# Moving the transposes of the merged branch sum behind the next twelve products in a two-layer mixer kernel

## Chip, cores and metric

The program runs on one core of one Trainium2 chip. The metric is the device time of one execution in microseconds (us); lower is better. TensorE (PE) does the matrix products and the transposes, VectorE (DVE) and ScalarE (ACT) the elementwise work, SyncE (SP) issues the loads of weights.

## What is computed

Two blocks follow one another, each with two layers, on 256 tokens of width 1024. Only the end of each layer of the second block matters here:

```python
merged = None
for n, yb in enumerate((y_hg, y_cf, y_sc, y_at, y_mem)):
    term = jax.nn.sigmoid(h @ w_gate[l, n]) * (yb @ w_branch[l, n])
    merged = term if merged is None else merged + term
x = x + rmsnorm(merged @ w_out[l], norm_post[l])
```

So five gated branches are summed into `merged` (256 x 1024), and the sum is multiplied by a 1024 x 1024 matrix.

## The kernel before, in words

Every large product is done in three passes on split operands: a value is cut into a high part (`wh`, `hh`, `yh`, `mh`) and a low part (`wl`, `hl`, `yl`, `ml`), and `mm3` adds high x high, high x low and low x high in PSUM (lines L527 to L529). The split of a tile is an ACT copy (high part) and a DVE subtraction (low part): L313 and L314 for weights, L533 and L534 (`split`) for activations. Weights arrive as 1 MB tiles `raw` from SP (L292), with three tiles in flight, and three pairs `wh`/`wl` in use. `ws.pace()` issues two half tiles of splitting after each step.

A branch is four steps of `chunk5` for the columns 0 to 511 (i = 0) and four for 512 to 1023 (i = 1). A step `part(q, t)` is twelve products, 4 slices of the contraction by 3 passes, each 128 x 512: q says which half of the contraction (one weight tile each), t which 128 of the 256 tokens. In the order of the branches the steps are (q, t) = (0,0), (0,1), (1,0), (1,1). A step with q = 1 finishes a gate and calls its `evac`, here `after(i)`: ACT takes tanh of the gate (`th`, L1725), PE multiplies the branch by its 1024-wide matrix (`br`, six products), DVE forms the term (L1736) and adds it to `m` (L1737), the token-major sum.

In the last branch (`pos == 4`) the sum is complete after each such call. It has to be transposed, since the product with `w_out` contracts over its columns: PE transposes 4 squares of 128 x 128 into one PSUM bank `tr` (L1742), and `split` makes `mh` and `ml` of them. I call these four groups of four transposes the turns: the first turn is (t, i) = (0, 0), the second (1, 0), the third (0, 1), the fourth (1, 1). Each layer has four, so the kernel has eight. Behind the fourth come the steps of the product with `w_out`, from `mh` and `ml`, in the order (0,0), (1,0), (0,1), (1,1) for the first 512 columns (`t_first=True`).

A scheduler places the instructions; on each engine they then run in the order that it has written.

Of the kernel before, what the change touches and what calls it, by code (L numbers as in the profile page):

```python
# [18 lines left out]
P = 128  # L19
# [327 lines left out]
def build(tc, a, out, dbg=None, stop=None):  # L347
# [11 lines left out]
    act, dve, pe = nc.scalar, nc.vector, nc.tensor  # L359

    def bank(name="ps"):
        return pp.tile([P, 512], F32, name=name, tag="ps")
# [5 lines left out]
    def row_bcast(ap, n):  # L368
        return bass.AP(tensor=ap.tensor, offset=ap.offset, ap=[[0, P], [1, n]])
# [17 lines left out]
    ident = cstt[:, 0:128]  # L387
# [3 lines left out]
    def pc(name, j=0, n=1):  # L391
        return pcol[:, PO[name] + j:PO[name] + j + n]
# [133 lines left out]
    def mm3(o, ah, al, bh, bl, start, stop):  # L526
        pe.matmul(o, ah, bh, start=start, stop=False, skip_group_check=True)  # L527
        pe.matmul(o, ah, bl, start=False, stop=False, skip_group_check=True)  # L528
        pe.matmul(o, al, bh, start=False, stop=stop, skip_group_check=True)  # L529

    def split(h, lo, src):

        act.activation(h, src, AF.Copy)  # L533
        dve.tensor_tensor(lo, src, h.bitcast(F32), op=OP.subtract)  # L534
# [91 lines left out]
    def views(key, nk=KD):  # L626
        wh, wl = ws.get(S[key])
        return (wh.rearrange("p (k c) -> p k c", k=nk), wl.rearrange("p (k c) -> p k c", k=nk))
# [16 lines left out]
    def chunk_steps(key, form, xs, evac):  # L645
# [3 lines left out]
        def half(i):  # L649
            def f():  # L650
                if i == 0:
                    box["ps"] = bank("mm").rearrange("p (i c) -> p i c", i=2)
                    box["w"] = views(key)
                for k in range(KD):
                    grp_k(box["ps"][:, i, :], form, box["w"], xs, i, k, KD, i == 0 and k == 0)
                if i == 1:
                    ws.done(S[key])
                    evac(box["ps"])
                ws.pace()
            return f  # L660
        return [half(0), half(1)]

    def chunk5(keys, xs, evac, t_first=False):


        box = {}

        def part(q, t):
            def f():
                if q == 0:  # L670
                    box[t] = bank("mm")
                wh, wl = views(keys[q], 4)
                ts = slice(t * P, (t + 1) * P)
                for k in range(4):
                    j = 4 * q + k
                    mm3(box[t], xs[0][:, j, ts], xs[1][:, j, ts], wh[:, k, :], wl[:, k, :], j == 0, j == 7)
                if t == 1:
                    ws.done(S[keys[q]])
                if q == 1:
                    evac(t, box[t])  # L680
                ws.pace()
            return f
        return [part(q, t) for t in range(2) for q in range(2)] if t_first else [
            part(q, t) for q in range(2) for t in range(2)]
# [262 lines left out]
    def mixer(l):  # L947
# [180 lines left out]
        steps = []  # L1128
        steps += chunk_steps(("w1", l, 6), "A", H, ev_misc)
        steps += chunk5([("w1", l, 2), ("w1", l, 3)], H, ev_q("a"))  # L1130
        steps += chunk5([("w1", l, 4), ("w1", l, 5)], H, ev_vf)
        for c in range(2):
            steps += chunk_steps(("w1", l, 7 + c), "B", H, ev_to(qf[:, 2 * c:2 * c + 2, :], 0.125))
# [217 lines left out]
    def layer2(l, st):  # L1351
# [312 lines left out]
        kmajor5([keys["hf_f"], keys["hf_b"]], H2, ev_f)  # L1664
        steps = []
        steps += chunk5([keys["hi"], keys["akv"]], H2, ev_hi)
        steps += chunk_steps(keys["hq"], "B", H2, evs["hq"][1])
        steps.append(lambda: active.append(hgrn()))
# [9 lines left out]
        m = ap_.tile([P, 2, 1024], F32, name="m")  # L1678
        ap3 = tc.tile_pool(name="at3", bufs=1)
        ap3_ = ap3.__enter__()  # L1680
        mm_box = []
# [4 lines left out]
        def finish(g):  # L1686
            if g in active:
                for _ in g:
                    pass
                active.remove(g)  # L1690

        def branch_steps(pos, n):
            box = {}

            def begin():
                if n in (3, 4):
                    finish(gens["at"])
                if n == 1:
                    finish(gens["cf"])
                if pos == 4:  # L1700
                    ap3.__exit__(None, None, None)
                    mp = tc.tile_pool(name="mh2", bufs=1)
                    mp_ = mp.__enter__()
                    mm_box.extend([mp, mp_.tile([P, KD, T], F32R, name="mh"), mp_.tile([P, KD, T], F32R, name="ml")])
                    gb = mp_.tile([P, 1024], F32, name="gb")
                    nc.scalar.dma_start(gb, row_bcast(a["npost"][l:l + 1], 1024))
                    xt = x_tok
                    if l == 0:
                        xt = mp_.tile([P, 2, 1024], F32, name="xt")
                        for t in range(2):  # L1710
                            for q in range(2):
                                b = bank("tr")
                                for j in range(4):
                                    pe.transpose(b[:, j * P:(j + 1) * P], x[:, 4 * q + j, t * P:(t + 1) * P], ident)
                                act.activation(xt[:, t, q * 512:(q + 1) * 512], b, AF.Copy)
                    mm_box.extend([xt, gb])
                yh = ap_.tile([P, 2, T], F32R, name="yh", bufs=1)
                yl = ap_.tile([P, 2, T], F32R, name="yl", bufs=1)
                split(yh, yl, sz[YN[n]])
                box["y"] = (yh, yl)  # L1720

            def after(i):
                def f(t, ps):
                    th = ap_.tile([P, 512], F32, name="th", bufs=2)
                    act.activation(th, ps, AF.Tanh, scale=0.5)  # L1725
                    b = bank("br")
                    wh, wl = views(("wbr", l, n), 2)
                    yh, yl = box["y"]
                    ts, s = slice(t * P, (t + 1) * P), slice(i * 512, (i + 1) * 512)
                    for k in range(2):  # L1730
                        mm3(b, yh[:, k, ts], yl[:, k, ts], wh[:, k, s], wl[:, k, s], k == 0, k == 1)
                    mm = m[:, t, s]
                    if pos == 0:
                        dve.scalar_tensor_tensor(mm, th, 1.0, b, op0=OP.add, op1=OP.mult)
                    else:
                        dve.scalar_tensor_tensor(th, th, 1.0, b, op0=OP.add, op1=OP.mult)  # L1736
                        dve.tensor_tensor(mm, mm, th, op=OP.add)  # L1737
                    if pos == 4:
                        mh, ml = mm_box[1:3]
                        b = bank("tr").rearrange("p (k c) -> p k c", k=4)  # L1740
                        for k in range(4):
                            pe.transpose(b[:, k, :], m[:, t, i * 512 + k * P:i * 512 + (k + 1) * P], ident)  # L1742
                        split(mh[:, 4 * i:4 * i + 4, ts], ml[:, 4 * i:4 * i + 4, ts], b)
                    if i == 1 and t == 1:
                        ws.done(S["wbr", l, n])
                return f
            out_ = []
            for i in range(2):
                cs = chunk5([("wgate", l, n, 2 * i), ("wgate", l, n, 2 * i + 1)], H2, after(i))
                if i == 0:  # L1750
                    first = cs[0]

                    def f0(first=first):
                        begin()
                        first()
                    cs[0] = f0
                out_ += cs
            return out_
# [8 lines left out]
        mp, mh, ml, xt, gb = mm_box  # L1767
# [33 lines left out]
        if l == 0:  # L1801

            mem_kv(1)
            with tc.high_priority(HP):
# [4 lines left out]
                for k in range(KD):  # L1809
                    g, b = pc("npre1", k), bs[k // 2][:, k % 2, :]  # L1810
# [31 lines left out]
```

## Time and profile before

| | |
|---|---|
| median of 3 runs | 1530.48 us (1529.31 to 1531.53) |
| the profiled execution | 1530.64 us, of which its span is 1528.7 us |
| PE busy, weight loads busy | 1457.7 us (95%), 1301.0 us (85%) |
| DVE, ACT busy | 1123.4 us (73%), 783.9 us (51%) |
| TensorE clock granted, mean over the span | 0.983 of full speed |

The span is the time from the first to the last instruction of the profiled execution. A busy share is an average over stages; which engine sets the end is read from the waits and from the chain of work that ended last.

### The profile page before, as it was taken

The numbers are of one execution on the slowest core, as the hardware profiler recorded it, in microseconds if no ns is written. First come the engines' busy times: TensorE is split into PE (matmuls) and PEld (weight loads), VectorE is DVE, ScalarE is ACT, GpSimd is POOL, SyncE is SP. The second block draws the span as 40 slices with busy tenths as digits, with TensorE's granted clock in tenths as the row PEclk, the third lists the DMA queues.
The fourth block names the chain that finished last, engine by engine and source line by source line (L and its number), as shares of the span: only waits on it lengthen the run. The fifth ranks groups of instructions, "written<-read, shape, count | busy, mean of one in ns | idle before, by whom it ended". The sixth has DMA issues, their size and how long they took to land.

```text
span 1528.7 us, 24737 instructions
## 1 busy us (share of the span) xinstructions
PE 1457.7 (95%) x10036; PEld 1301.0 (85%) x10036; DVE 1123.4 (73%) x1983; ACT 783.9 (51%) x1310; POOL 18.0 (1%) x21
## 2 busy tenths in 40 slices
PE   3999998999989999999999999999998999999997
PEld 1688797999978887989999999987886898977875
DVE  7887565798977876778866777976665759976654
ACT  2655543655655555465555564346454754455442
POOL 0000000000000000000000000000000000000000
PEclk9999999999999999999999999999999999999999
DMA  9567534678744665557655352254553542435541
GB/s 366 204 237 268 193 138 143 248 267 297 263 165 138 248 221 193 193 195 270 228 191 194 138 193 101 95 191 139 182 217 116 215 160 89 159 117 181 190 165 55
DMA packets 42451, 289.21 MB, mean 189 GB/s; under 512 B 4993, under 2 KB 6145, under 8 KB 8034
## 3 DMA queue, kind: packets, MB, share of 16 engines
q1 hardware_dynamic: 39456, 281.77, 51.4%
q10 hardware_dynamic: 2882, 5.88, 1.1%
q8 instruction: 78, 1.28, 0.3%
q14 instruction: 35, 0.29, 0.1%
HBM read 285.53 MB, written 2.10 MB: 188 GB/s over the span
## 4 chain that ended last, share of the span: by engine, by line
PE 80%; DVE 6%; DMA 2%; ACT 2%; issue 1%; POOL 1%; DVEq 0%; POOLq 0%; ACTq 0%; SPq 0%
PE mm L528 20%; PE mm L527 19%; PE mm L529 19%; PE acc L528 2%; PE acc L529 2%; PE acc L527 2%; DVE wl L314 1%; PE br L529 1%; PE br L527 1%; PE br L528 1%; DVE cc L1626 1%; PE S L1477 1%; PE tr L781 1%; ACT wh L313 1%; PE ex L1498 1%
## 5 line engine op out<-in xcount | busy, mean ns | idle before, releaser
L314 DVE TENSOR_TENSOR wl<-raw,wh 128x1024 fp32r<-128x1024 f32 x428 | 515.3, 1219 | 183.4 <-ACT wh L313 180.8
L313 ACT ACTIVATE wh<-raw 128x1024 fp32r<-128x1024 f32 x428 | 440.2, 1054 | 345.8 <-PE mm L528 212.7
L528 PE MATMUL mm<-hl,wh 128*128 128x256 f32 x1568 | 451.2, 288 | 0.0
L527 PE MATMUL mm<-hh,wh 128*128 128x256 f32 x1568 | 448.1, 286 | 2.3 <-ACT wh L313 2.3
L529 PE MATMUL mm<-hh,wl 128*128 128x256 f32 x1568 | 448.0, 286 | 2.2 <-DVE wl L314 2.2
L528 PEld LDWEIGHTS mm<-hl,wh 128*128 128x128 f32 x1568 | 302.3, 193 | 8.2 <-issue 7.1
L527 PEld LDWEIGHTS mm<-hh,wh 128*128 128x128 f32 x1568 | 302.3, 193 | 6.2 <-ACT wh L313 2.5
L529 PEld LDWEIGHTS mm<-hh,wl 128*128 128x128 f32 x1568 | 302.1, 193 | 3.7 <-DVE wl L314 3.0
L528 PE MATMUL mm<-wl,hh 128*128 128x512 f32 (+1 forms) x496 | 194.9, 393 | 0.0
L527 PE MATMUL mm<-wh,hh 128*128 128x512 f32 (+1 forms) x496 | 192.9, 389 | 1.1 <-ACT hh L598 1.1
L529 PE MATMUL mm<-wh,hl 128*128 128x512 f32 (+1 forms) x496 | 192.0, 388 | 1.6 <-DVE hl L534 1.6
L528 PEld LDWEIGHTS mm<-wl,hh 128*128 128x128 f32 x496 | 94.3, 190 | 23.3 <-issue 4.5
L527 PEld LDWEIGHTS mm<-wh,hh 128*128 128x128 f32 x496 | 94.5, 191 | 21.1 <-ACT hh L598 1.4
L529 PEld LDWEIGHTS mm<-wh,hl 128*128 128x128 f32 x496 | 94.4, 190 | 19.6 <-DVE hl L534 1.8
L418 DVE SCALAR_TENSOR_TENSOR raw<-raw,cbp 128x1024 f32<-128x1024 f32 x80 | 96.1, 1218 | 9.5 <-DMA raw<-in_modw 9.3
L528 PE MATMUL acc<-zl,wh 128*128 128x256 f32 x352 | 98.3, 280 | 0.6 <-DVE zl L534 0.6
L529 PE MATMUL acc<-zh,wl 128*128 128x256 f32 x352 | 98.5, 280 | 0.0
L527 PE MATMUL acc<-zh,wh 128*128 128x256 f32 x352 | 98.4, 281 | 0.0
L528 PEld LDWEIGHTS acc<-zl,wh 128*128 128x128 f32 x352 | 66.3, 188 | 1.0 <-DVE zl L534 1.0
L527 PEld LDWEIGHTS acc<-zh,wh 128*128 128x128 f32 x352 | 66.0, 188 | 0.2
L529 PEld LDWEIGHTS acc<-zh,wl 128*128 128x128 f32 x352 | 66.1, 188 | 0.0
L752 ACT ACTIVATE p<-lg,nm 128x256 f32<-128x256 f32 (+1 forms) x80 | 33.5, 430 | 46.3 <-DVE nm L749 46.3
(409 smaller groups left out, 2073.1 us busy)
## 6 DMA issues: line engine op xcount, KB each, us to landing
raw<-in_w SPq DMA_DIRECT2D x70, 1024.0 KB, 4.9
raw<-in_wup SPq DMA_DIRECT2D x44, 1024.0 KB, 4.9
raw<-in_modw SPq DMA_DIRECT2D x40, 1024.0 KB, 5.0
raw<-in_wgate SPq DMA_DIRECT2D x40, 1024.0 KB, 4.8
raw<-in_wdn SPq DMA_DIRECT2D x22, 1024.0 KB, 4.8
raw<-in_wo SPq DMA_DIRECT2D x16, 1024.0 KB, 4.8
raw<-in_wbr SPq DMA_DIRECT2D x10, 1024.0 KB, 4.8
gst<-in_modw SPq DMA_DIRECT2D x8, 1024.0 KB, 12.7
```

Of the source, the lines that this page charges most:

```text
L313: nc.scalar.activation(h[:, s], r[:, s], AF.Copy)
L314: nc.vector.tensor_tensor(lo[:, s], r[:, s], h[:, s].bitcast(F32), op=OP.subtract)
L418: dve.scalar_tensor_tensor(v, v, 1.0, cb_box[0], op0=OP.mult, op1=OP.mult, accum_out=col)
L527: pe.matmul(o, ah, bh, start=start, stop=False, skip_group_check=True)
L528: pe.matmul(o, ah, bl, start=False, stop=False, skip_group_check=True)
L529: pe.matmul(o, al, bh, start=False, stop=stop, skip_group_check=True)
L752: act.activation(p4[:, h, 0:nk], src[:, i, 0:nk], AF.Exp, bias=nm[:, h:h + 1], accum_out=su[:, h:h + 1])
L781: pe.transpose(b[:, h, :], p4[:, h, kt * P:(kt + 1) * P], ident)
L1477: pe.matmul(b[par][:, 2 * s + ft, :], kt[r, ft, s * P:(s + 1) * P], qt[r, ft, t * P:(t + 1) * P], start=True, stop=True, skip_group_check= ...
L1498: pe.matmul(o, g[:, d, t, ft * P:(ft + 1) * P], cols[0], start=(t == 0 and n == 0), stop=(n == 1), skip_group_check=True)
L1626: dve.scalar_tensor_tensor(c[:, ft, :], u[:, ft, k:k + T], w, c[:, ft, :], op0=OP.mult, op1=OP.add)
```

## The change

The transposes of a turn and the split of what they give become a function `turn`, put on a list `late` and called by the next step of `chunk5`, after its twelve products and ahead of its `evac`. The first and the third turn were scheduled into the middle of the following step's products before; now they stand behind all twelve. The second turn stood directly behind the six `br` products that complete its sum; now the first step (0,0) of the columns 512 to 1023 stands between. The fourth turn goes behind the first step of the product with `w_out`, which needs only tokens 0 to 127 and columns 0 to 511, that is the first turn's result. No operation is added or taken away.

```diff
+    late = []
+
     def chunk5(keys, xs, evac, t_first=False):
...
                 if t == 1:
                     ws.done(S[keys[q]])
+                while late:
+                    late.pop(0)()
                 if q == 1:
                     evac(t, box[t])
                 ws.pace()
...
                     if pos == 4:
-                        mh, ml = mm_box[1:3]
-                        b = bank("tr").rearrange("p (k c) -> p k c", k=4)
-                        for k in range(4):
-                            pe.transpose(b[:, k, :], m[:, t, i * 512 + k * P:i * 512 + (k + 1) * P], ident)
-                        split(mh[:, 4 * i:4 * i + 4, ts], ml[:, 4 * i:4 * i + 4, ts], b)
+                        def turn():
+                            mh, ml = mm_box[1:3]
+                            b = bank("tr").rearrange("p (k c) -> p k c", k=4)
+                            for k in range(4):
+                                pe.transpose(b[:, k, :], m[:, t, i * 512 + k * P:i * 512 + (k + 1) * P], ident)
+                            split(mh[:, 4 * i:4 * i + 4, ts], ml[:, 4 * i:4 * i + 4, ts], b)
+                        late.append(turn)
```

The order of the instructions on PE at the second turn of the first layer, before: `br_11811` is the branch product that completes the sum, `tr_11820` the turn, `mm_11835` the next gate.

```order
L528 MATMUL br_11811<-wl_11681,yh_11721 128x512
L529 MATMUL br_11811<-wh_11680,yl_11722 128x512
L1742 MATMUL tr_11820<-cstt_78,m_10711 128x128 x4
L527 MATMUL mm_11835<-wh_11759,hh_135 128x512
L528 MATMUL mm_11835<-wl_11760,hh_135 128x512
```

The same place in the changed kernel (the new lines push the transposes to L1748, and `mm_11828` is the same gate under another number):

```order
L529 MATMUL br_11811<-wh_11680,yl_11722 128x512
L527 MATMUL mm_11828<-wh_11759,hh_135 128x512
L528 MATMUL mm_11828<-wl_11760,hh_135 128x512
...
L529 MATMUL mm_11828<-wh_11759,hl_136 128x512
L1748 MATMUL tr_11841<-cstt_78,m_10711 128x128 x4
L527 MATMUL mm_11848<-wh_11759,hh_135 128x512
```

The twelve products of one step, four times L527 to L529, have come in between. At the fourth turn PE had, before, with `br_11913` as the last branch product and `mm_11940` the first bank of the product with `w_out`:

```order
L528 MATMUL br_11913<-wl_11681,yh_11721 128x512
L529 MATMUL br_11913<-wh_11680,yl_11722 128x512
L1742 MATMUL tr_11922<-cstt_78,m_10711 128x128 x4
L527 MATMUL mm_11940<-wh_11861,mh_11692 128x512
L528 MATMUL mm_11940<-wl_11862,mh_11692 128x512
```

and has in the changed kernel:

```order
L529 MATMUL br_11913<-wh_11680,yl_11722 128x512
L527 MATMUL mm_11933<-wh_11861,mh_11692 128x512
...
L529 MATMUL mm_11933<-wh_11861,ml_11693 128x512
L1748 MATMUL tr_11946<-cstt_78,m_10711 128x128 x4
L527 MATMUL mm_11933<-wh_11922,mh_11692 128x512
```

Here too the turn has moved behind twelve products; the product behind it takes the second weight tile of `w_out`. On ACT the tanh of the second gate has moved ahead of the first turn's high part; before:

```order
L1725 ACTIVATE th<-mm 128x512
L533 ACTIVATE mh<-tr 128x4x128
L1725 ACTIVATE th<-mm 128x512
L313 ACTIVATE wh<-raw 128x1024 x2
L533 ACTIVATE mh<-tr 128x4x128
```

and in the changed kernel:

```order
L1730 ACTIVATE th<-mm 128x512 x2
L533 ACTIVATE mh<-tr 128x4x128
L313 ACTIVATE wh<-raw 128x1024 x2
L533 ACTIVATE mh<-tr 128x4x128
L313 ACTIVATE wh<-raw 128x1024 x2
```

The order on DVE, POOL and SP is the same in both kernels.

## Rows read from the trace of the kernel before

**Rows 1.** The page, chain of work that ended last: shares of the span by engine

```profile
PE 80%; DVE 6%; DMA 2%; ACT 2%; issue 1%; POOL 1%; DVEq 0%; POOLq 0%; ACTq 0%; SPq 0%
```

**Rows 2.** Waits of PE from 1136 to 1529 us: total, times, longest

```profile
PE tr L1742 <- DVE m L1737: 10.4, 4, 2.7
```

**Rows 3.** Timeline, first layer's second turn: start, length, instruction, idle before and releaser

```profile
1143.30 0.66 PE L1742 MATMUL tr<-cstt,m 128*128 128x128 f32 x4
...
1144.62 0.69 DVE L534 TENSOR_TENSOR ml<-tr,mh 128x512 fp32r<-128x512 f32 x1 [1.38 <-ACT mh L533]
...
1145.15 0.60 ACT L1725 ACTIVATE th<-mm 128x512 f32<-128x512 f32 x1 [0.56 <-PE mm L529]
...
1146.11 0.40 PE L529 MATMUL br<-wh,yl 128*128 128x512 f32 x1
1146.62 0.69 DVE L1736 SCALAR_TENSOR_TENSOR th<-th,br 128x512 f32<-128x512 f32 x1 [1.30 <-PE br L529]
1147.22 1.22 DVE L314 TENSOR_TENSOR wl<-raw,wh 128x1024 fp32r<-128x1024 f32 x1
1148.36 0.69 DVE L1737 TENSOR_TENSOR m<-m,th 128x512 f32<-128x512 f32 x1
...
1149.19 1.08 PE L1742 MATMUL tr<-cstt,m 128*128 128x128 f32 x4 [2.68 <-DVE m L1737]
...
1153.99 0.39 PE L527 MATMUL mm<-wh,hh 128*128 128x512 f32 x1
```

**Rows 4.** Timeline, first layer's third and fourth turn and the product behind

```profile
1162.23 0.39 PE L527 MATMUL mm<-wh,hh 128*128 128x512 f32 x1
...
1163.31 0.39 PE L529 MATMUL mm<-wh,hl 128*128 128x512 f32 x1
...
1165.41 0.40 PE L529 MATMUL br<-wh,yl 128*128 128x512 f32 x1
...
1166.52 1.22 DVE L314 TENSOR_TENSOR wl<-raw,wh 128x1024 fp32r<-128x1024 f32 x1
...
1168.26 2.35 DVE L314 TENSOR_TENSOR wl<-raw,wh 128x1024 fp32r<-128x1024 f32 x2
...
1168.40 0.65 PE L1742 MATMUL tr<-cstt,m 128*128 128x128 f32 x4 [2.59 <-DVE m L1737]
...
1169.13 0.39 PE L528 MATMUL mm<-wl,mh 128*128 128x512 f32 x1
...
1173.24 0.39 PE L527 MATMUL mm<-wh,mh 128*128 128x512 f32 x1
...
1176.04 0.39 PE L527 MATMUL mm<-wh,mh 128*128 128x512 f32 x1
```

**Rows 5.** Busy time by stretch: us and instructions of each engine, granted PE clock, DMA

```profile
1149.20:1152.40 3.20, 3.20 (x10) 2.72 (x11) 1.67 (x2) 0.60 (x1) 0.00 (x0) 0.50 0.40 67
...
1499.20:1502.20 3.00, 3.00 (x16) 2.47 (x15) 3.00 (x4) 0.66 (x2) 0.00 (x0) 1.00 0.00 0
1288.00:1296.00 8.00, 7.44 (x56) 7.22 (x57) 8.00 (x17) 2.80 (x5) 0.00 (x0) 0.79 0.09 37
```

**Rows 6.** Timeline of PE, second layer's second and fourth turn

```profile
1476.63 0.40 PE L529 MATMUL br<-wh,yl 128*128 128x512 f32 x1
...
1484.44 0.39 PE L527 MATMUL mm<-wh,hh 128*128 128x512 f32 x1
...
1495.85 0.40 PE L529 MATMUL br<-wh,yl 128*128 128x512 f32 x1
...
1502.13 0.40 PE L527 MATMUL mm<-wh,mh 128*128 128x512 f32 x1
```

**Rows 7.** Timeline of SP, issue of the second layer's first weight tiles

```profile
1186.44 71.47 SPq L292 DMA_DIRECT2D raw<-in_w  x13
```

**Rows 8.** The page, DMA issues: count, size, median us to landing

```profile
raw<-in_w SPq DMA_DIRECT2D x70, 1024.0 KB, 4.9
```

## Prediction, made before the changed kernel ran

> **What bounds the kernel now.** I read the chain of work that ended last first, then who PE waits for, then the timeline around those waits, and last the granted clock.
>
> PE carries 80% of the chain [rows 1], so time that PE spends idle or slow is time of the kernel as long as nothing later waits for something else. From 1136 us to the end PE waits for DVE at the turns (L1742) four times, 10.4 us in all and 2.7 us at most [rows 2]. The four are the second and the fourth turn of each layer. The timeline shows why [rows 3]: the last branch product starts at 1146.11, DVE forms the term from 1146.62, splits half a weight tile (L314, 1.22 us, standing between the two DVE steps of the sum), adds to `m` from 1148.36, and the transposes start at 1149.19, after 2.68 us idle. From the last branch product to the turn that is 3.08 us here and 1168.40 - 1165.41 = 2.99 us at the fourth turn [rows 4]. Twelve products whose operands were ready stood behind the waiting turn, and none of them ran.
>
> The wait has a second price. In the 3.2 us behind the first layer's second turn the granted clock is 0.50, which is 1.2 GHz, and only 10 PE instructions fit in; behind the second layer's fourth turn it is 1.00, 2.4 GHz, with 16 in 3.0 us [rows 5]. The idle time ahead was about the same, so the fall does not always come: here behind three of the four waits.
>
> By the Trainium skill, page "TensorE: Matmul & The Clock Gate", Part 1, the engine's clock falls to half when PE idles and comes back with activity, and its phase isn't tied to the start of the kernel, so that the number of slow products differs from run to run. The three falls of four in this trace agree with it. Taken strictly, with four falls in a typical run, before would lose some 1.6 us more than in the profiled run; time after would not change by it.
>
> **The change, part by part.** Nothing is added or removed. I price a turn and a step where they run undisturbed at full clock. Twelve products take 1176.04 - 1173.24 = 2.80 us, 0.23 each [rows 4]. A turn adds 0.50: from its start at 1168.40 to the second product behind it at 1169.13 are 0.73 us, and 0.23 of these are one product [rows 4].
>
> *Second and fourth turns.* Without a wait or a low clock the thirteenth product behind the branch products would start 0.23 + 0.50 + 2.80 = 3.53 us after the last of these, whether the turn stands before or behind the twelve. What it starts later is the loss:
> - first layer, second turn: 1146.11 + 3.53 = 1149.64, in the trace 1153.99: 4.35 us [rows 3]
> - first layer, fourth turn: 1165.41 + 3.53 = 1168.94, in the trace 1173.24: 4.30 us [rows 4]
> - second layer, second turn: 1476.63 + 3.53 = 1480.16, in the trace 1484.44: 4.28 us [rows 6]
> - second layer, fourth turn: 1495.85 + 3.53 = 1499.38, in the trace 1502.13: 2.75 us [rows 6]
>
> Together 15.68 us. The last one has only the wait in it; in the others the low clock adds some 1.55 us.
>
> What is left of the waits: the sum needs 3.08 or 2.99 us from the last branch product, and PE now has 0.23 + 2.80 = 3.03 us of work there. So 0.05 us stay at the first place and nothing at the others, whose idle time is below the longest (10.4 us over four is 2.60 on average [rows 2], against 2.80 of new cover). With no idle time I expect no low clock there either. This cover is nearly exact: each 0.1 us that the sum comes later shows as 0.1 us of wait.
>
> *First and third turns.* They stood in the middle of a step. From the product ahead of the third turn to the second behind it are 1163.31 - 1162.23 = 1.08 us [rows 4]; two products and a turn make 0.96, so 0.12 us were a wait for `m`. Five more products, 1.17 us, now stand ahead: the wait is gone. The first turns look the same, so four times 0.12 = 0.48 us.
>
> *Does the moved split delay the sum?* On DVE the low part `ml` of the first turn stands ahead of the term of the second. Its turn now starts after five more products, less the 0.12: 1143.30 + 1.05 = 1144.35. `ml` followed the turn by 1144.62 - 1143.30 = 1.32 us, so it runs from 1145.67 to 1146.36 [rows 3]. The tanh that now goes ahead of the high part on ACT took from 1145.15 to 1145.75; its gate is finished 0.62 us earlier (turn and wait stand no longer in it), so it ends at 1145.13, as the first turn's result arrives. The term can start at 1146.62 - 0.12 = 1146.50. So `ml` is out of the way by 0.14 us: nothing, with a thin margin.
>
> *Weights.* The twelve products in the gap use a tile that was split before; the step behind the fourth turn takes the next. Its first low half is ready at 1166.52 + 1.22 - 0.12 = 1167.62, and PE wants it in the second product of that step, at about 1169.1; the second half ends about 1169.3 (the first of the two from 1168.26) and is wanted about 1170.4 [rows 4]. Margins of 1.4 and 1.1 us, so no wait.
>
> *Further on.* The second layer then begins 8.65 + 0.24 - 0.05 = 8.8 us earlier. That is kept if the loads move along. Thirteen of its tiles are issued within 71.47 us, 71.47 / 12 = 6.0 us apart [rows 7], and land 4.9 us after issue [rows 8]. So the loads wait for free buffers, not for the memory, and follow PE.
>
> **Sum.** 15.68 + 0.48 - 0.05 = 16.1 us. The profiled execution took 1530.64 us, so it becomes 1514.5; its time was 0.16 above the median of the runs, and I forecast 1514.4 us. Since time after contains none of the four low stretches, it hangs little on how many a run of before had.
>
> **The rivals.**
> - *The wait comes back in part.* The cover is exact to about 0.1 us, and the margin for `ml` is 0.14. If the sum comes later by a whole ACT step and a whole DVE step, 0.60 + 0.69 = 1.29 us [rows 3], at each of the four turns, 5.2 us return: 1519.7. Against it: the order on DVE is unchanged, and each of its steps starts from a branch product that is no later. The loads could also give back the first layer's 8.8 us, 1523.3, but have 1.1 us of slack for each tile. Together 13%, most of it below 1518.5.
> - *The low clock goes elsewhere.* In the second layer there is another low stretch: in the 8 us from 1288 the mean granted clock is 0.79, and PE is idle for 0.56 us of them [rows 5]. It may move or vanish when all comes 8.8 us earlier: 1.55 us either way, 1513.0 or 1516.1. The trace can't decide it. 15%, both ways alike. What the Trainium skill says of the phase (Part 1, above) speaks for this rival.
> - *Nothing changes.* If PE could pass a waiting turn, the order would not matter: 1530.5. PE stood still for 2.68 us with ready products behind [rows 3], so 2%.
> - *Slower.* PE arrives at the second weight tile of the output product ahead of its split. At this place each us that the half comes later beyond the margin costs one, at each of four turns if the gates' tiles were late too. It decides against the change when the halves come 16.1 / 4 + 1.1 = 5.1 us later than in the rows, and at 6 us later the time would be 1534. DVE and ACT have the same work in the same stretch, so 2%.
>
> **How the numbers follow.** The forecast has 68%, the partial wait 13%, the clock elsewhere 15%, no change 2%, slower 2%. The forecast alone spans 1513.5 to 1515.7 (one wait of 0.1 us and the spread of a turn's price more or less). The range to 1512.0 takes in the clock's better side with the runs' scatter of about 1 us, and to 1518.5 its worse side and most of the partial wait; outside remain no change, slower and the heavy partial waits. A change within 0.2%, 3.1 us, can't be told from none with this kernel. Faster by more than that is everything up to 1527.4: 95%; same 3%; slower 2%.
>
> **What would show it.** In the profile after: PE's wait for `m` at the turns (L1748 there) falls from 10.4 us in four to below 0.5; the granted clock behind the four turns is 1.00; twelve products stand between the last branch product and the turn, 0.23 us apart; the turn still adds 0.50. The first layer's wo2 steps come about 8.8 us earlier and the second layer's end 16. I am wrong if PE waits for `ml` or a weight half behind the fourth turn, if the term starts behind a late `ml`, or if the second layer doesn't start 8.8 us earlier.

## The result and the profile after

The changed kernel takes **1511.86 us** (median of 4 runs, 1509.73 to 1512.97) against 1529.89 us (4 runs, 1527.58 to 1531.53, three of them the runs that the forecast knew) of the kernel before: a ratio of **0.9883** [0.9872, 0.9895], 18.0 us faster. The forecast was 1514.4, and the median lies 0.14 us under the lower end of the range. The profiled execution took 1512.37 us, with a span of 1510.6 us and a mean granted clock of 0.986 (0.983 before).

The page of the profile after, busy times and the chain that ended last; the second line answers to [rows 1]:

```profile
PE 1451.8 (96%) x10036; PEld 1298.5 (86%) x10036; DVE 1123.4 (74%) x1983; ACT 782.3 (52%) x1310; POOL 18.4 (1%) x21
...
PE 81%; DVE 7%; ACT 2%; DMA 1%; issue 1%; POOL 1%; DVEq 0%; POOLq 0%; ACTq 0%
```

PE is the bound as it was. Waits of PE from 1136 us to the end (total, times, longest), which answers to [rows 2]:

```profile
PE S L1482 <- DVE K L1523: 3.4, 4, 1.9
PE tr L1815 <- ACT m L1802: 0.9, 1, 0.9
PE rb L1559 <- DVE yb__13447 L1555: 0.2, 1, 0.2
```

The turns (L1748 now) are no longer among them. The timeline at the first layer's second turn, which answers to [rows 3]:

```profile
1139.18 0.40 PE L527 MATMUL br<-wh,yh 128*128 128x512 f32 x1
...
1143.34 0.60 PE L1748 MATMUL tr<-cstt,m 128*128 128x128 f32 x4
...
1144.01 0.39 PE L528 MATMUL br<-wl,yh 128*128 128x512 f32 x1
...
1144.65 0.69 DVE L534 TENSOR_TENSOR ml<-tr,mh 128x512 fp32r<-128x512 f32 x1 [2.38 <-ACT mh L533]
...
1144.93 0.39 PE L529 MATMUL br<-wh,yl 128*128 128x512 f32 x1
...
1145.36 0.69 DVE L1741 SCALAR_TENSOR_TENSOR th<-th,br 128x512 f32<-128x512 f32 x1
...
1147.10 0.69 DVE L1742 TENSOR_TENSOR m<-m,th 128x512 f32<-128x512 f32 x1
...
1147.68 0.39 PE L529 MATMUL mm<-wh,hl 128*128 128x512 f32 x1
...
1147.93 0.63 PE L1748 MATMUL tr<-cstt,m 128*128 128x128 f32 x4
1148.32 0.48 PE L527 MATMUL mm<-wh,hh 128*128 128x512 f32 x1
...
1150.93 0.39 PE L529 MATMUL mm<-wh,hl 128*128 128x512 f32 x1
```

The last branch product starts at 1144.93 and the turn at 1147.93, 3.00 us later (3.08 before [rows 3]); but twelve products now lie between. The sum is finished at 1147.10 + 0.69 = 1147.79, and the turn starts 0.14 us later. That is no slack: while PE stood waiting in the kernel before, the same 0.14 us passed between the end of the sum, 1148.36 + 0.69 = 1149.05, and the turn at 1149.19 [rows 3]. The turn starts 0.25 us behind the product ahead of it, where a step between products is 0.23, so at most 0.02 us are a wait, and the cover is as exact as it was forecast. The fourth turn of the layer, with the 24th product behind its branch products, answers to [rows 4]:

```profile
1159.63 0.39 PE L529 MATMUL br<-wh,yl 128*128 128x512 f32 x1
...
1162.66 0.60 PE L1748 MATMUL tr<-cstt,m 128*128 128x128 f32 x4
1163.02 0.48 PE L527 MATMUL mm<-wh,mh 128*128 128x512 f32 x1
1163.33 0.39 PE L528 MATMUL mm<-wl,mh 128*128 128x512 f32 x1
...
1165.66 0.39 PE L529 MATMUL mm<-wh,ml 128*128 128x512 f32 x1
```

Busy time by stretch, with the granted clock third from the end, behind the same turns as in [rows 5] (first layer's second and fourth, second layer's fourth) and, in the last row, 8 us around the place that lay behind 1288:

```profile
1147.90:1151.10 3.20, 3.20 (x17) 2.74 (x17) 1.72 (x2) 0.60 (x1) 0.00 (x0) 1.00 0.33 74
1162.70:1166.10 3.40, 3.40 (x18) 2.85 (x17) 3.40 (x4) 1.01 (x3) 0.00 (x0) 1.00 0.44 94
1483.60:1486.60 3.00, 3.00 (x17) 2.49 (x16) 3.00 (x4) 1.01 (x2) 0.00 (x0) 1.00 0.00 0
1277.00:1285.00 8.00, 6.58 (x62) 6.47 (x63) 8.00 (x17) 3.46 (x6) 0.00 (x0) 1.00 0.17 71
```

The clock is full behind the turns, and also in the last stretch, where it was 0.79 before. (That window lies 0.85 us ahead of the work of the window from 1288, so only the clock is compared there, not the busy times.)

**Where the time came from.** A layer's stretch is measured here from the first product of the branch group ahead of its first turn (1139.18 after) to the 24th product behind the branch group of its fourth (1165.66): 26.48 us. It is cut at the last product of the second and fourth branch group (1144.93, 1159.63) and the 24th product behind the second (1150.93), so that each piece holds one turn. The same was read off every trace of this study (us):

| kernel | stretch starts | first layer: 1st, 2nd, 3rd, 4th turn | second layer | from the one to the other | behind | span |
|---|---|---|---|---|---|---|
| before | 1140.16 | 5.95, 10.38, 8.92, 10.40 | 5.96, 10.30, 8.92, 8.84 | 294.86 | 24.01 | 1528.7 |
| after | 1139.18 | 5.75, 6.00, 8.70, 6.03 | 5.75, 5.93, 8.70, 6.05 | 294.50 | 24.01 | 1510.6 |

Of the 18.1 us between the spans, the second and fourth turns give 4.38 + 4.37 + 4.37 + 2.79 = 15.91, the first and third 0.20 + 0.22 + 0.21 + 0.22 = 0.85, the way from one layer to the other 0.36, and 0.98 arose ahead of the first moved instruction, where the two programs are the same. So 16.76 us are shown to come from the moved turns; the last two parts are looked at below.

### The profile page after: what moved, and what is told of

It is laid out like the page before. It is cut to its first block, busy times and chain, and to the rows that moved or that the text cites. A ratio compares the mean times of both kernels' runs of the same rounds, so it can differ in the third digit from the quotient of the medians.

```text
span 1510.6 us, 24733 instructions
## 1 busy us (share of the span) xinstructions
PE 1451.8 (96%) x10036; PEld 1298.5 (86%) x10036; DVE 1123.4 (74%) x1983; ACT 782.3 (52%) x1310; POOL 18.4 (1%) x21
## 3 DMA queue, kind: packets, MB, share of 16 engines
q8 instruction: 78, 1.28, 0.3%
## 4 chain that ended last, share of the span: by engine, by line
PE 81%; DVE 7%; ACT 2%; DMA 1%; issue 1%; POOL 1%; DVEq 0%; POOLq 0%; ACTq 0%
PE mm L528 20%; PE mm L527 20%; PE mm L529 19%; PE acc L528 3%; PE acc L529 3%; PE acc L527 3%; DVE cc L1631 2%; DVE wl L314 1%; PE br L527 1%; PE br L528 1%; PE br L529 1%; PE tr L786 1%; PE ob L1117 1%; DMA ohf<-in_onehot 1%; PE lg L1106 1%
## 5 line engine op out<-in xcount | busy, mean ns | idle before, releaser
L527 PE MATMUL mm<-hh,wh 128*128 128x256 f32 x1568 | 448.7, 287 | 2.2 <-ACT wh L313 2.2
L529 PE MATMUL mm<-hh,wl 128*128 128x256 f32 x1568 | 448.7, 286 | 1.2 <-DVE wl L314 1.2
L527 PEld LDWEIGHTS mm<-hh,wh 128*128 128x128 f32 x1568 | 302.8, 193 | 6.0 <-ACT wh L313 2.4
L529 PEld LDWEIGHTS mm<-hh,wl 128*128 128x128 f32 x1568 | 302.7, 193 | 2.4 <-DVE wl L314 1.7
L527 PE MATMUL mm<-wh,hh 128*128 128x512 f32 (+1 forms) x496 | 192.1, 388 | 1.1 <-ACT hh L598 1.1
L529 PE MATMUL mm<-wh,hl 128*128 128x512 f32 (+1 forms) x496 | 191.5, 386 | 1.6 <-DVE hl L534 1.6
L527 PEld LDWEIGHTS mm<-wh,hh 128*128 128x128 f32 x496 | 93.9, 189 | 20.8 <-ACT hh L598 1.4
L529 PEld LDWEIGHTS mm<-wh,hl 128*128 128x128 f32 x496 | 93.8, 189 | 19.5 <-DVE hl L534 1.8
L529 PE MATMUL acc<-zh,wl 128*128 128x256 f32 x352 | 98.7, 281 | 0.0
L527 PE MATMUL acc<-zh,wh 128*128 128x256 f32 x352 | 98.5, 281 | 0.0
L527 PEld LDWEIGHTS acc<-zh,wh 128*128 128x128 f32 x352 | 66.2, 189 | 0.2
L529 PEld LDWEIGHTS acc<-zh,wl 128*128 128x128 f32 x352 | 66.2, 188 | 0.0
L1730 ACT ACTIVATE th<-mm 128x512 f32<-128x512 f32 x40 | 23.8, 596 | 70.3 <-PE mm L529 70.3
```

## The experiments

The theory: a turn ahead of ready products costs PE the wait for the sum, about 2.8 us, and, where the clock falls behind it, some 1.55 us more; the change removes both at the second and fourth turns. The rivals: the gain lies in the first and third turns as well or instead; the low clock has causes elsewhere, so that its share would not follow the waits; part of the gain is the spread of one execution. All kernels were timed in five rounds, and the kernel before beside them. The diffs are against the changed kernel where nothing else is said.

| kernel | median us (lowest to highest) | beside it, before | ratio |
|---|---|---|---|
| second and fourth turns late | 1513.06 (1511.95 to 1514.77) | 1528.67 | 0.9900 [0.9886, 0.9913] |
| first and third turns late | 1528.17 (1526.09 to 1530.35) | 1528.67 | 0.9998 [0.9989, 1.0007] |
| before with 12 filling products | 1523.22 (1522.20 to 1524.67) | 1528.67 | 0.9966 [0.9953, 0.9978] |
| before with 6 filling products | 1523.02 (1522.36 to 1524.89) | 1528.67 | 0.9967 [0.9955, 0.9980] |
| before again | 1529.52 (1527.49 to 1531.05) | 1529.00 | 1.0000 [0.9991, 1.0010] |
| after again | 1511.57 (1511.23 to 1513.14) | 1529.00 | 0.9887 [0.9874, 0.9901] |
| turns late in the first layer | 1522.09 (1520.19 to 1524.10) | 1529.00 | 0.9954 [0.9941, 0.9966] |
| turns made twice | 1516.76 (1515.80 to 1518.31) | 1529.00 | 0.9920 [0.9906, 0.9934] |
| norms filled, 4 + 2 | 1516.40 (1515.18 to 1516.89) | 1528.72 | 0.9916 [0.9901, 0.9932] |
| norms filled, 5 + 5 | 1519.38 (1518.90 to 1520.31) | 1528.72 | 0.9938 [0.9924, 0.9951] |
| norms filled, 2 + 1 | 1508.87 (1507.87 to 1510.13) | 1528.75 | 0.9870 [0.9853, 0.9886] |
| after, a third time | 1511.91 (1510.60 to 1514.82) | 1528.75 | 0.9891 [0.9876, 0.9906] |

**Second and fourth turns alone.**

```diff
-                        late.append(turn)
+                        if t == 1:
+                            late.append(turn)
+                        else:
+                            turn()
```

> Only the second and the fourth turn of each layer are moved; the first and the third stand in the middle of a step as before. Theory A (the gain is the four waits of PE for the sum, and the low clock behind three of them): about 15.7 us of the gain stay, so 15.5 to 17.5 us below the kernel before, within 1 us of the full change. Theory B (the first and third turns carry a good part, since the full change gained 18.0 us and the waits only explain 15.7): 2 us or more are missing, at most 16 us below before. In the trace by theory A the wait for the sum is below 0.5 us in all and the granted clock behind the four places is 1.00.

Measured: 1513.06 us, 15.6 us faster than before, at the lower end of what theory A expected, and 1.2 to 1.5 us above the first two medians of the full change. In the trace the pieces with the moved turns fell to 6.09, 6.04, 6.04 and 6.04 us; those with the first and third turns stayed at 5.95 and 8.90. The two layers' stretches are 1.0 us longer than in the changed kernel, so the first and third turns carry that much and not the 2 us of theory B. Nearly all of the gain is in the second and fourth turns.

**First and third turns alone.**

```diff
-                        late.append(turn)
+                        if t == 0:
+                            late.append(turn)
+                        else:
+                            turn()
```

> Only the first and the third turn are moved, the second and fourth stand directly behind the branch products as before. Theory A: about 0.5 us faster (four times 0.12 us), which this measurement can't tell from no change; the waits stay at 10 to 10.5 us in four places and the low clock comes behind some of them. Theory B: 2 us or more faster.

Measured: 1528.17 us, a ratio that includes no change. In the trace the four pieces are 5.75, 8.71, 5.75 and 8.70 us, 0.84 us less than before together, and the waits of PE are those of [rows 2]:

```profile
PE tr L1748 <- DVE m L1742: 10.3, 4, 2.6
```

So the earlier turns are worth 0.8 us, which the timing of the whole kernel can't show. The pieces with the second and fourth turns were 10.32, 8.85, 10.17 and 10.38 us: three are long again, but the short one is now the first layer's fourth, which was long before. The fall of the clock belongs to the waits, and at which of them it stays away changes.

**Products to fill the wait, the turns left where they were.** Products on operands that lie ready, into a bank that nothing reads, ahead of the second and fourth turns. Against the kernel before:

```diff
+                    if pos == 4 and t == 1:
+                        d = bank("fill")
+                        for k in range(4):
+                            mm3(d, yh[:, k % 2, ts], yl[:, k % 2, ts], wh[:, k % 2, s], wl[:, k % 2, s], k == 0, k == 3)
```

> The kernel before, with twelve products more at each of the four waits: they go into a PSUM bank that nobody reads, directly behind the branch products, so that PE works while it would have waited. They take 12 x 0.23 = 2.8 us, the wait was 2.6 us. Theory A splits the loss into 2.6 us of wait and about 1.55 us of low clock at three of four places: the waits stay as lost time, the low stretches go, so 4.0 to 6.2 us faster than before, with a granted clock of 1.00 behind all four. Rival C (the low clock there has nothing to do with the idle time and only happens to fall there): the low stretches stay, and the time is that of before or up to 0.5 us longer.

The other has half as many, `range(2)` and `k == 1`:

> The same with six products instead of twelve: PE works for 1.4 us of each wait and idles for the other 1.2 us. Theory A: the sum arrives as before, so where the clock does not fall behind 1.2 us of idle time the time is that with twelve, 4 to 6 us below before; where it still falls behind all, the time is that of before. Rival C: as before.

Measured: 1523.22 and 1523.02 us, 5.5 and 5.7 us faster than before, although one does 48 and the other 24 products more than it. Twelve products fill the wait (timeline of the first layer's second turn, PE):

```profile
1145.43 0.40 PE L529 MATMUL fill<-wh,yl 128*128 128x512 f32 x1
1145.71 0.63 PE L1746 MATMUL tr<-cstt,m 128*128 128x128 f32 x4
```

Six leave 1.28 us of it:

```profile
1144.90 0.40 PE L529 MATMUL fill<-wh,yl 128*128 128x512 f32 x1
...
1146.57 0.63 PE L1746 MATMUL tr<-cstt,m 128*128 128x128 f32 x4 [1.28 <-DVE m L1741]
```

In its waits of PE the turns are still there, with half the time of [rows 2]:

```profile
PE tr L1746 <- DVE m L1741: 5.0, 4, 1.3
```

The four pieces are 8.81, 8.90, 8.75 and 8.90 us with twelve and 8.81, 8.91, 8.73 and 8.90 with six; the one undisturbed piece of before was 8.84. So a place without the fall takes 8.8 to 8.9 us whether PE idles or works on products for nothing, and a fall adds 10.38 - 8.81 = 1.57 us (1.50 and 1.55 at the other two places where before had one). The two layers' stretches together got 4.4 to 4.5 us shorter; the rest of the 5.5 and 5.7 lies outside them, where the runs scatter. In the 3.2 us behind the turn the granted clock was 1.00 with twelve and, after 1.28 us idle, with six as well:

```profile
1146.50:1149.70 3.20, 3.13 (x16) 2.68 (x17) 1.75 (x2) 0.60 (x1) 0.00 (x0) 1.00 0.38 69
```

Neither of the two traces has a stretch of lower clock behind any of its turns, so rival C, a low clock that only happens to fall there, is out. The two parts of the gain are thereby measured apart: the clock, 1.50 to 1.57 us at each place where it fell, and the wait, 8.84 - 6.05 = 2.79 us at the one place of before without a fall and 2.8 to 2.9 at the others against the filled kernel. Useful work in the wait got both, work for nothing got the first alone.

**The same two kernels again**, for the spread of a run. No edit.

> The kernel before once more, for a second profile. By the profiled run on which the sum rests, three low stretches behind the four waits and a time of 1530.6 us; the fifteen runs of it in the comparison with the parts of the change had a median of 1528.7. Theory A with a run-to-run scatter from the clock: the four waits are again 10 to 10.5 us, the number of low stretches behind them is 2 to 4, and the stretch ahead of the first turn starts within 2 us of the earlier profile, with all of that difference made by low stretches elsewhere. Rival D (the profiled run was typical and the scatter is something else): three low stretches at the same places, and the difference ahead of the first turn without one.

> The changed kernel once more, beside the kernel before on the same chip in the same rounds. Theory A: the local terms are 15.7 us for the second and fourth turns and 0.5 to 1.0 us for the first and third, so 16 to 17.5 us below before. If the change really gains 18 us as in its first four runs (rival E, a gain elsewhere, between the places), it is again 17.5 to 18.5 us below.

Measured: 1529.52 against 1529.00 us for the kernel before, ratio 1.0000; 1511.57 us for the changed one, 17.4 us below the 1529.00 and 18.0 below the 1529.52. The first is at the upper end of theory A, the second what rival E expected, so the times decide for neither. In the second trace of before the clock falls behind the same three waits, as both of its expectations allowed. In the traces the two layers' stretches repeat: 35.65 and 34.04 us for before (35.65 and 34.02 in the first trace), 26.49 and 26.45 for after (26.48 and 26.43). What doesn't repeat is the time at which the first stretch starts. In the eleven traces of kernels whose code is the same up to there, it starts between 1136.68 and 1140.67 us. In the three that started first, at 1136.68, 1137.52 and 1137.55, the mean granted clock from 20 to 1135 us was 0.986; in the eight others, which started from 1138.36 on, 0.982 to 0.985. In two of the three the time at half clock behind the norms near 661 and 866 us is shorter than in the nine other traces, and the lead over the first trace of before grows by 1.1 to 1.5 us at each of the two. So the clock makes part of this scatter, but not all: the first trace of the changed kernel started 0.98 us earlier than that of before at a lower mean clock (0.983 against 0.985). What makes the rest stays open.

**The turns late in the first of the two layers only.**

```diff
-                        late.append(turn)
+                        if l == 0:
+                            late.append(turn)
+                        else:
+                            turn()
```

> The turns are moved in the first of the two layers only. Theory A (each place for itself, and what comes later moves along): 8.8 to 9.4 us below before, two waits of 2.6 us left in the second layer, and all of the second layer starts some 9 us earlier. Rival F (the loads or a DVE-bound stretch between the places give part of it back): less than 8 us.

Measured: 1522.09 us, 6.9 us faster than before, less than I expected. The first layer's stretch is 26.49 us, which is the whole gain of 9.16 there, and the loads follow (1460.69 - 1139.35 = 321.34 us from the one layer's first branch product to the other's, 330.51 before). But the second layer's stretch, whose code was as before, took 35.62 us instead of 34.02: its fourth turn, the one place of before without a fall, had one now. Its pieces are 5.97, 10.32, 8.93 and 10.40. In this profiled run 1.6 us of the gain went to the clock at a wait that was left in; nothing was given back between the layers, against rival F. How far the clock explains the median of the five runs is not shown, since only this one has a trace.

**Each turn made twice,** the second time over the first, at the new place.

```diff
-                            for k in range(4):
+                            for k in (0, 1, 2, 3, 0, 1, 2, 3):
```

> The changed kernel with every turn done twice into the same bank: eight transposes instead of four, the same result. It prices a turn that does not come out of a wait. At 0.10 us for each transpose that follows another, 8 x 0.4 = 3.1 us more than the changed kernel; if the 0.50 us of the prediction were the price of four transposes without any fixed part, 8 x 0.5 = 4.0 us more.

Measured: 1516.76 us, 5.2 us more than the changed kernel beside it, above both expected values. In the trace the two stretches are 28.45 and 28.37 us, 3.91 more than after, or 0.49 for each of the eight turns added; the other 1.3 us are not in the stretches and not explained (single runs of this kernel lie up to 2.5 us apart). PE at the first layer's third turn:

```profile
1158.01 0.39 PE L529 MATMUL mm<-wh,hl 128*128 128x512 f32 x1
1158.24 1.03 PE L1748 MATMUL tr<-cstt,m 128*128 128x128 f32 x8
1159.03 0.48 PE L527 MATMUL br<-wh,yh 128*128 128x512 f32 x1
1159.35 0.39 PE L528 MATMUL br<-wl,yh 128*128 128x512 f32 x1
```

From its start to the second product behind are 1.11 us, 0.88 without one product; in the kernel after it is 1144.01 - 1143.34 - 0.23 = 0.44 for a single turn. Between products the price is proportional to the transposes, with no fixed part that could be saved by gathering turns. The mean of 0.49 is above 0.44 mostly because the pieces with the second turns grew by 0.57. The turn came 0.39 us behind the product ahead of it there, where a step is 0.23, so 0.16 us were a wait, and again it came 0.14 us behind the end of the sum (1148.45):

```profile
1148.20 0.39 PE L527 MATMUL mm<-wh,hh 128*128 128x512 f32 x1
1148.59 1.07 PE L1748 MATMUL tr<-cstt,m 128*128 128x128 f32 x8
```

**Filling another wait.** If the clock falls behind a wait like those at the turns, other waits should be open to the same cure. In the norms PE waits for POOL's factor four times, 7.7 us in all. The changed kernel, with discarded products on values that are ready at that time, four behind the first value and two behind the second, in five norms:

```diff
+    def fill(v, n):
+        f = bank("fill")
+        for i in range(n):
+            pe.matmul(f[:, 0:T], v[:, 0:1].to_broadcast([P, P]), cstt[:, 0:T], start=(i == 0), stop=(i == n - 1),
+                      skip_group_check=True)
...
-        y = rstd(st.ps[:, 0:2], 2, 1.0 / 1024, "rs")
+        y = rstd(st.ps[:, 0:2], 2, 1.0 / 1024, "rs", box=vbox)
+        fill(vbox.pop(), 4)
...
+        fill(y, 2)
```

> The changed kernel, with six discarded products more in each of the five norms (four after the sum of squares, two after the broadcast of its root), where PE waits for DVE, POOL and ACT and the granted clock is low for 3 to 10 us in every profile so far. Theory A carried over (idle time of PE ahead of products costs clock as well, and work in it keeps the clock): 2 to 8 us faster than the changed kernel, with fewer low stretches between 240 and 960 us. Rival G (there DVE and ACT are the bound, so PE's clock costs nothing): the same as the changed kernel, or up to 2 us longer by the fill in the way.

With five and five, to see the price of the fill itself:

> The same with five and five discarded products. Theory A carried over: at least as few low stretches as with four and two; where the five behind the broadcast reach into the time in which the first products are ready they cost up to 0.4 us each, so 2 us better to 4 us worse than with four and two. Rival G: longer than with four and two, 1 to 5 us.

Measured: 1516.40 and 1519.38 us, slower than the changed kernel by at least 4.5 and 7.5 (its medians were 1511.57 to 1511.91, measured on other chips). With four and two both expectations were missed: theory A had forecast a gain, rival G at most 2 us of loss. Five and five were 3.0 us slower than four and two, which both expectations allowed. The mean granted clock from 20 to 1135 us was 0.988 and 0.989, above the 0.983 to 0.986 of the three traces of the changed kernel, so the loss does not come from the clock: the fill was too long. One wait of PE after, then the same place with four:

```profile
661.04 1.22 PE L550 MATMUL rb<-cstt,rsy 128*128 128x128 f32 x4 [2.15 <-POOL rsy L544]
```

```profile
661.13 2.99 PE L819 MATMUL fill<-cstt,rsv 128*128 128x256 f32 x8 [0.42 <-DVE rsv L541]
663.91 1.06 PE L552 MATMUL rb<-cstt,rsy 128*128 128x128 f32 x4
```

The first fill takes 2.99 us where PE had waited for 2.15, and `rb`, which the norm needs, stands behind it: from the second product group `st` to `rb` it took 663.91 - 660.10 = 3.81 us, against 661.04 - 658.28 = 2.76 in the changed kernel.

**The norms with a short fill**: two and one instead of four and two, in four norms.

```diff
-        fill(vbox.pop(), 4)
+        fill(vbox.pop(), 2)
...
-        fill(y, 2)
+        fill(y, 1)
```

> The changed kernel with two discarded products after the sum of squares and one after the broadcast, in four of the five norms. With four and two the fill itself took 2.5 to 3.8 us where PE had waited 1.1 to 2.2, and pushed the broadcast back. Two take about 1.3 us and fit. Theory A carried over: no broadcast is later and some low stretches go, 1 to 4 us faster than the changed kernel (1511.7). Rival G: within 1 us of it.

> The changed kernel a third time, on the same chip as the small fill, to compare with it. As before: 16 to 18 us below the kernel before, median 1511 to 1513; the stretch ahead of the first turn begins anywhere between 1136 and 1141 us.

Measured: **1508.87 us**, against 1511.91 of the changed kernel on the same chip in the same rounds; the two sets of runs don't overlap (the first set of the changed kernel, with 1509.73 to 1512.97, does overlap with the 1507.87 to 1510.13 of this one). The expectation for the changed kernel was met: 16.8 us below before, and its stretch started at 1137.55. At the place above:

```profile
658.35 1.13 PE L819 MATMUL fill<-cstt,rsv 128*128 128x256 f32 x4 [0.42 <-DVE rsv L541]
660.09 1.23 PE L552 MATMUL rb<-cstt,rsy 128*128 128x128 f32 x4 [0.61 <-POOL rsy L546]
```

The fill ends ahead of POOL's factor, so `rb` starts when it would have anyway: again 2.76 us behind the second group `st`, at 657.33 in this trace. This version is 1.3% under the kernel before and 0.2% under the changed one. The mean granted clock from 20 to 1135 us was 0.989, and 1.94 of the 2.0 us between its trace and the third trace of the changed kernel arise ahead of the first turn. That fits theory A, but it is one trace against code that scatters by 4 us there; which of the four norms gives what was not taken apart.

## Why the prediction came out as it did, point by point

- **What bounds the kernel, and the twelve products behind the turn: right.** The wait for `m` is gone but for some 0.02 us, the granted clock is 1.00 behind the turns, and the four places gave 15.91 us against 15.68. Moving those turns alone gave 15.6 us of the whole.
- **The left-over wait of 0.05 us: right in kind, at most 0.02.** The sum came as late as PE could bear. The forecast let the term start behind the last branch product as late as before; it started 1145.36 - 1144.93 = 0.43 us behind it, 0.51 before [rows 3].
- **The price of a turn: 0.06 us too high, so the gain too small.** I took 0.50 for a turn, from one that started after idle time [rows 4]; a turn between products costs 0.44: 1143.34 to 1144.01 and 1162.66 to 1163.33 are both 0.67 us, less 0.23 for one product. All eight turns stand between products now. At the second and fourth turns four times 0.06 is the 0.24 by which 15.68 was too small. At the first and third turns 0.85 us were gained instead of 0.48. The third turn of before, and behind it that of after with the product ahead of it:

```profile
1162.58 0.66 PE L1742 MATMUL tr<-cstt,m 128*128 128x128 f32 x4
```

```profile
1157.80 0.39 PE L529 MATMUL mm<-wh,hl 128*128 128x512 f32 x1
1158.03 0.60 PE L1748 MATMUL tr<-cstt,m 128*128 128x128 f32 x4
```

  The product ahead of the turn started at 1162.23 [rows 4], so 0.35 us lay between them before and 0.23 lie there now: the wait was the 0.12 that I had worked out. With the cheaper turn it makes 0.18 of the 0.20 to 0.22 that each place gained.
- **The split `ml` ahead of the term: right, by less than forecast.** It ends at 1145.34 and the term starts at 1145.36: it isn't late, but 0.02 us lie between them and not 0.14.
- **The weights: right.** PE waits for no half of a tile behind the fourth turn.
- **Further on: right.** The second layer's first branch product came 1470.67 - 1460.16 = 10.51 us earlier, of which 0.98 were there ahead of the change and 0.36 fell on the way; the 9.17 of the first layer were kept in full, where 8.8 had been worked out.
- **The rival that the low clock goes elsewhere: it happened, at another price.** The low stretch near 1289 vanished. I priced it 1.55 us, like one behind a turn; the way between the layers became 0.36 us shorter. DVE is busy for 8.00 of the 8 us there [rows 5], and PE at full clock waits for it: its waits for DVE's `K` grew from 2.5 us in two to 3.4 in four (the line after stands above). Before:

```profile
PE S L1477 <- DVE K L1518: 2.5, 2, 1.9
```

  In the traces of all fourteen runs this way takes either 294.38 to 294.50 us, in eight of them, or 294.79 to 294.91, in six. The six have one low stretch there and two waits for `K`, the eight have no low stretch and four waits. Kernels with the turns late stand in both groups, so the 0.36 us are luck of the run and not shown to be a gain of the change.
- **The step that failed: the base and its scatter.** "The profiled execution took 1530.64 us, so it becomes 1514.5; its time was 0.16 above the median of the runs". I took one execution and three runs for the kernel's time, and 1 us for the scatter. In the four later sets of 15, 15, 9 and 7 runs the kernel before had medians of 1528.67, 1529.00, 1528.72 and 1528.75 us, and single runs from 1526.05 to 1531.50; a fifth set, of 11 runs, had 1529.52. The profiled one was 1.6 to 2.0 us above the first four medians and 1.1 above the fifth. With 1528.8 for the base, the unchanged sum of 16.1 gives 1512.7, and with the terms that measured larger (0.23 at the second and fourth turns, 0.37 at the others, 0.05 of wait that hardly came) 1512.0, beside medians of 1511.57 to 1511.91. So the mechanism held. Of the 2.5 us between forecast and median the base made 1.7 and the terms some 0.65; why one run of before takes longer than another is shown only in part (above).

The account of the two profiled executions closes in the same way: 1514.53 - 1512.37 = 2.16 us that the sum missed are 0.65 for those three terms, 0.36 between the layers, 0.98 ahead of the change, and 0.17 outside the span (1.94 us before, 1.77 after).

By the Trainium skill, page "TensorE: Matmul & The Clock Gate", Part 1, the number of slow products differs from run to run since the gate's phase is not tied to the kernel. The traces agree: in four of them with the turns left in place, 11 of 14 waits of 2.5 to 2.7 us were followed by a fall, and not always at the same places. The prediction's four falls "taken strictly" came in no trace; the three with all four waits had three falls each. The rule would have been a reason for a wider base in the prediction, and I used it only for the stretches that the change moves.

## What to carry to other kernels

In a kernel that one engine bounds, an instruction that waits in its queue ahead of ready work costs the wait and, as PE showed here behind 11 of 14 waits, often the clock behind it; moving it behind as much ready work as the wait is long gained both here, and the sum can be read from two rows at each place. Where there is no useful work, a few products for nothing kept the clock here, but they must end before what PE waits for arrives: three in each of four norms gained 3.0 us, six in each of five lost 4.5. For the absolute time take the median of many runs as the base, since the very same code arrived at the changed place up to 4 us apart.

## What was not expected of the hardware

- A wait of 1.3 us, with products ahead of it, was not followed by a lower granted clock at any of four places, while waits twice as long mostly were (11 of 14, above).
- Four 128x128 transposes of f32 back to back cost PE 0.44 us between products, eight cost 0.88; four that started after idle time cost 0.50 (1168.40 to 1169.13 less one product [rows 4]).
- A stretch at a granted clock of 0.50 cost 1.50 to 1.57 us where PE was the bound, and 0.4 us between the layers, where PE waited for DVE (six traces with it against eight without).
